# Norms without a shift folded into weights and outputs: x transposed instead of the normalised h

## The chip, the cores and the metric

The kernel runs on 1 core of one Trainium2 chip. The metric is the device time of one execution in microseconds; a comparison uses the median of several runs. The profile is one execution recorded by the hardware profiler.

## What is computed

256 rows of 1024 numbers, x, go through two blocks, each two layers deep. A layer of the first block is an FFN, a token mixer with three branches (retention, latent attention, differential attention), cross attention to a memory, and a second FFN. The second block has adaptive norms, a hybrid mixer and a mixture of experts; its parts stay as they are. What matters here is the norm ahead of each part of the first block:

```python
def rms_norm(x, gain=None):
    y = xf * lax.rsqrt(jnp.mean(xf * xf, axis=-1, keepdims=True) + EPS)
    if gain is not None:
        y = y * gain
...
for l in range(DEPTH):
    h = rms_norm(x, ffn1_norms[l, 0])
    x = x + 0.5 * rms_norm(swiglu(h, ffn1_w13[l], ffn1_w2[l]), ffn1_norms[l, 1])
    h = rms_norm(x, mix_norms[l, 0])
    y = token_mixing(h, w_in[l], ...)
    x = x + rms_norm(y, mix_norms[l, 1])
    h = rms_norm(x, cross_norms[l, 0])
    m = rms_norm(mem, cross_norms[l, 2])
    x = x + rms_norm(cross_attention(h, m, ...), cross_norms[l, 1])
    h = rms_norm(x, ffn2_norms[l, 0])
    x = x + 0.5 * rms_norm(swiglu(h, ffn2_w13[l], ffn2_w2[l]), ffn2_norms[l, 1])
```

In such a norm a row of x is multiplied by its own inverse root and then, column by column, by a gain. The result goes into a matrix product: h @ w.

## The kernel before

**Precision and weights.** Products are made in three passes of a 4-byte format: an operand is split into a high part and the low rest, and high x high, high x low and low x high are summed in PSUM (mm3, lines 288 to 290). Weights come from HBM in packages of 1 MB (mostly four k-slices of 128 rows and 512 columns) into one of four raw buffers. A class Stream holds the list of all packages in their order of use. Its pump splits them ahead of use into a ring of eight places (four tiles named hl, two tiles named pair that hold two splits each): ScalarE copies the slice into the high part (line 276), VectorE subtracts to get the low part (line 278). At a few packages, the first of a stage, every second low part is made by GpSimd instead. A place is free again when PE has done the matmuls of its split.

**Stages.** TensorE's order is written out by hand in the program's order; every engine takes its instructions in order. In a dense stage (dense) each k-slice gives six matmuls, three for each of the two tiles of 128 rows. After each stage's output product (dense_out) stands a boundary. At dense_out's end eight splits are kept: row tile 0 runs all of them first, and rest then gives out the eight parts of row tile 1 (three matmuls each) between the steps of the boundary.

**A boundary** (boundary, from line 516) does for each row tile: squares of the output y on ScalarE (line 444), y times its gain on VectorE (491, 493), the inverse root by a sum on VectorE (449) and a power on GpSimd (450), x plus the scaled y (496); this is add_post. Then pre_norm: squares of x (444), its root (449, 450), and h = x times root times gain (512). Then to_fm transposes h by eight matmuls against an identity (431) into two PSUM tiles, and hilo splits these: hh on ScalarE (282), hl on VectorE (283). Then the first projection of the next stage (staggered, 358 and 360) uses the eight splits of its first two packages: for each half of four k-slices, eight matmuls with hh and then four with hl. It runs wholly for row tile 0, and then for row tile 1, whose pre_norm and transposes stand in between. The order of calls for row tile 0: add_post, pre_norm, the last five parts of rest, transposes. The gain of each norm comes by a DMA that spreads one row over 128 partitions.

Between mix and cross attention, a boundary hands its steps to a filler: they are issued between the k-slices of the memory's projections. The boundaries into the second block have a shift in their norm.

**Stages ahead and behind.** An FFN has eleven blocks of its up projection (w13) with SiLU and a product (696, 697); in eight of them VectorE also accumulates the modulation vectors of the second block (1310, 1312). Mix copies projections from PSUM by evacuate (731), has sigmoids (1043, 1095), and normalises the latent vectors (qn, 875) before they are transposed (431).

## Time and profile before

| what | value |
|---|---|
| median of 3 runs | 2259.35 us (2256.45 to 2260.48) |
| profiled execution, its own time | 2260.74 us |
| its span, first to last instruction | 2258.9 us |
| mean granted TensorE clock | 0.976 |
| busy: PE, DVE, ACT, POOL | 94%, 60%, 49%, 5% |
| HBM read | 554.14 MB |

PE is TensorE with its matmuls, PEld its weight loads, DVE VectorE, ACT ScalarE, POOL GpSimd. A row of the timeline has its start, its length, the engine, the line, the operation, what is written and read, the number of instructions merged, and in brackets the idle time before it and what ended it. A row of groups has the count, the busy time and the mean of one in ns. The waits say which line waited for which. The stage table has one row for each stretch of time.

### The profile page before, as it was taken

The numbers are of one execution on the slowest core, as the hardware profiler recorded it, in microseconds if no ns is written. First come the engines' busy times: TensorE is split into PE (matmuls) and PEld (weight loads), VectorE is DVE, ScalarE is ACT, GpSimd is POOL, SyncE is SP. The second block draws the span as 40 slices with busy tenths as digits, with TensorE's granted clock in tenths as the row PEclk, the third lists the DMA queues.
The fourth block names the chain that finished last, engine by engine and source line by source line (L and its number), as shares of the span: only waits on it lengthen the run. The fifth ranks groups of instructions, "written<-read, shape, count | busy, mean of one in ns | idle before, by whom it ended". The sixth has DMA issues, their size and how long they took to land. (4 is left out here: it accounts for less than half of the span.)

```text
span 2258.9 us, 28926 instructions
## 1 busy us (share of the span) xinstructions
PE 2122.5 (94%) x10668; PEld 1565.5 (69%) x10668; DVE 1347.0 (60%) x2468; ACT 1097.0 (49%) x2194; POOL 103.1 (5%) x100
## 2 busy tenths in 40 slices
PE   7999999999999999999999999998989886999885
PEld 6887878888788788777788878876765333775341
DVE  5876667764776677676678568766562114563111
ACT  5544666565554455465756555545842112753110
POOL 1001000000100100010000010002000001000000
PEclk9999999999999999999999999999999798999998
DMA  8875534553576577744356437766479998568998
GB/s 287 310 246 188 210 117 167 202 196 128 207 282 241 197 273 259 255 175 150 132 196 212 166 118 273 259 239 239 165 285 377 419 420 314 217 228 340 419 418 344
DMA packets 95705, 557.26 MB, mean 247 GB/s; under 512 B 11096, under 2 KB 13083, under 8 KB 42551
## 3 DMA queue, kind: packets, MB, share of 16 engines
q1 hardware_dynamic: 95550, 555.28, 66.4%
q8 instruction: 88, 1.44, 0.3%
q14 instruction: 67, 0.54, 0.1%
HBM read 554.14 MB, written 1.10 MB: 246 GB/s over the span
## 5 line engine op out<-in xcount | busy, mean ns | idle before, releaser
L278 DVE TENSOR_TENSOR hl<-raw,hl 128x512 fp32r<-128x512 f32 (+2 forms) x586 | 392.5, 685 | 129.9 <-ACT hl L276 124.5
L276 ACT ACTIVATE hl<-raw 128x512 fp32r<-128x512 f32 (+1 forms) x602 | 366.2, 627 | 206.8 <-PE y L290 62.4
L278 DVE TENSOR_TENSOR pair<-raw,pair 128x512 fp32r<-128x512 f32 (+2 forms) x468 | 305.0, 692 | 125.6 <-ACT pair L276 121.1
L276 ACT ACTIVATE pair<-raw 128x512 fp32r<-128x512 f32 x484 | 276.8, 622 | 184.4 <-PE gu L290 69.3
L1921 PE MATMUL gu<-raw,xg 128*32 128x512 f32 x1024 | 144.3, 635 | 28.3 <-DMA raw<-w_gu 26.4
L288 PE MATMUL gu<-pair,hh 128*128 128x512 f32 x320 | 127.6, 399 | 0.0
L288 PE MATMUL gu<-hl,hh 128*128 128x512 f32 x320 | 127.5, 398 | 0.0
L290 PE MATMUL gu<-hl 128*128 128x512 f32 x320 | 125.7, 393 | 0.0
L290 PE MATMUL gu<-pair,hl 128*128 128x512 f32 x320 | 125.1, 391 | 0.0
L289 PE MATMUL gu<-pair,hh 128*128 128x512 f32 x320 | 124.8, 390 | 0.0
L289 PE MATMUL gu<-hl,hh 128*128 128x512 f32 x320 | 124.8, 390 | 0.0
L1312 DVE SCALAR_TENSOR_TENSOR ada<-raw,cact,ada 128x512 f32<-128x512 f32 x168 | 122.2, 746 | 0.0
L1921 PEld LDWEIGHTS gu<-raw,xg 128*32 128x32 f32 x1024 | 29.7, 111 | 109.3 <-DMA raw<-w_gu 55.9
L1908 PEld LDWEIGHTS gather<-P,u 128*128 128x128 f32 x512 | 70.7, 218 | 29.2 <-issue 20.0
L1978 PE MATMUL dn<-raw,aT 128*32 128x512 f32 x512 | 77.9, 622 | 9.9 <-ACT xg L1913 2.8
L1961 DVE SCALAR_TENSOR_TENSOR sil<-sil,cs,gu 128x256 f32<-128x256 f32 x16 | 7.7, 480 | 127.4 <-ACT sil L1960 127.2
L1908 PE MATMUL gather<-P,u 128*128 128x128 f32 x512 | 76.5, 308 | 3.3 <-DVE xg L1915 1.9
L283 DVE TENSOR_TENSOR y<-dn,y 128x512 fp32r<-128x512 f32 x32 | 22.1, 692 | 92.7 <-ACT y L282 92.6
L450 POOL TENSOR_TENSOR rs<-rs_tmp,mhalf 128x1 f32<-128x1 f32 x44 | 25.6, 581 | 1131.2 <-DVE rs_tmp L449 1122.7
L1913 ACT ACTIVATE xg<-gather,fm 128x128 f32<-128x128 f32 x64 | 29.3, 457 | 98.3 <-PE gather L1908 83.8
L288 PE MATMUL y<-hl,ah 128*128 128x512 f32 x184 | 73.4, 399 | 0.0
L1915 DVE TENSOR_SCALAR xg<-gather,fm 128x128 f32<-128x128 f32 x64 | 26.2, 410 | 78.1 <-ACT xg L1913 74.0
(663 smaller groups left out, 4730.5 us busy)
## 6 DMA issues: line engine op xcount, KB each, us to landing
raw<-w SPq DMA_DIRECT2D x131, 1024.0 KB
raw<-w_gu SPq DMA_DIRECT2D x98, 1024.0 KB
raw<-win SPq DMA_DIRECT2D x71, 1024.0 KB
raw<-w_dn SPq DMA_DIRECT2D x54, 1024.0 KB
raw<-w_ada SPq DMA_DIRECT2D x48, 1024.0 KB
raw<-w_gu SPq DMA_DIRECT2D x60, 512.0 KB
raw<-w_out SPq DMA_DIRECT2D x16, 1024.0 KB
raw<-cross_wkv SPq DMA_DIRECT2D x16, 1024.0 KB
```

Of the source, the lines that this page charges most:

```text
L276: nc.scalar.activation(hi, raw[:, c0:c0 + n], AF.Copy)
L278: eng.tensor_tensor(out=lo, in0=raw[:, c0:c0 + n], in1=hi.bitcast(F32), op=ALU.subtract)
L288: te.matmul(out, xh, wh, start=start, stop=False)
L289: te.matmul(out, xh, wl, start=False, stop=False)
L290: te.matmul(out, xl, wh, start=False, stop=stop)
L450: self.nc.gpsimd.tensor_tensor(out=out, in0=tmp, in1=self.mhalf[:, 0:1], op=ALU.pow)
L1312: nc.vector.scalar_tensor_tensor(self.ada[:, c], w, act, self.ada[:, c], op0=ALU.mult, op1=ALU.add)
L1908: te.matmul(ps[:, (k - k0) * 128:(k - k0 + 1) * 128], hm[t][:, k * 128:(k + 1) * 128], P[t][:, q * 128:(q + 1) * 128], start=(t == 0), sto ...
L1913: nc.scalar.activation(xg[:, k, :], v, AF.Identity, bias=sh, scale=g)
L1915: ve.tensor_scalar(xg[:, k, :], v, g, sh, op0=ALU.mult, op1=ALU.add)
L1921: te.matmul(gu[32 * e:32 * e + 32, :], xg[:, k, 32 * e:32 * e + 32], w(e), start=(k == 0), stop=(k == 7))
L1978: te.matmul(dn[half][32 * e:32 * e + 32, :], aT[:, f, 32 * e:32 * e + 32], w(e), start=(f == 0), stop=(f == 1))
```

## The change

For the norms without a shift whose output goes into a product (FFN1, FFN2, mix and cross of both layers), h is no longer made. The gain of a norm belongs to the k rows of the weight. A table of all these gains, g_pre (128 x 64), is loaded once, and a split of w13, win, win_mla or cross_wq multiplies with its column: ScalarE's copy gets it as a scale vector, and VectorE computes raw times gain minus high part in one instruction. GpSimd makes none of these splits. The root of a row tile belongs to the rows of the product; it is put into a small tile, pre (128 x 2), and multiplied in where the projections leave PSUM: as the scale vector of SiLU, sigmoid, copies and squares, and in the product behind SiLU. In mix the latent's root is multiplied with it once more. x itself is transposed and split. The norm of the memory and the norms of the second block stay.

The order in a boundary changes too: x of row tile 0 is transposed after seven of the eight parts of rest, and the squares and roots of both tiles stand behind the transposes of tile 1.

```diff
+NORMED = {"w13_1": 0, "w13_2": 1, "win": 2, "win_mla": 2, "cross_wq": 3}
...
+            name, index, pool = self.keys[i]
+            gain = None
+            if name in NORMED:
+                k = 16 * NORMED[name] + 8 * index[0] + 4 * (index[1] % 2) + s
+                gain = self.kern.g_pre[:, k:k + 1]
+            self.ready.append((i, self.kern.split(place, self.raws[i], c0, w, pool and self.emitted % 2, gain)))
...
+        if gain is not None:
+            nc.scalar.activation(hi, raw[:, c0:c0 + n], AF.Copy, scale=gain)
+            nc.vector.scalar_tensor_tensor(lo, raw[:, c0:c0 + n], gain, hi.bitcast(F32), op0=ALU.mult, op1=ALU.subtract)
+            return hi, lo
...
+        fold = gn == FOLDED
+        if fold:
+            self.pre = self.small.tile([128, 2], F32, tag="pre", name="pre", bufs=2)
         def pre_of(t):
-            if gn is not None:
+            if fold:
+                ms = self.small.tile([128, 2], F32, tag="ms", name="ms")
+                for i, c in enumerate(HALF):
+                    self.square_sum(ms[:, i:i + 1], self.x[t][:, c], D, tiles[t][0][:, c])
+                self.rstd2(self.pre[:, t:t + 1], ms)
+            elif gn is not None:
                 self.pre_norm(self.x[t], gn[0], gn[1], *tiles[t])
...
-            self.to_fm(tiles[t][1], hT[t], 8)
+            self.to_fm(self.x[t] if fold else tiles[t][1], hT[t], 8)
...
-        pre_of(0)
-        rest(2, 2)
-        rest(4)
-        post_of(1)
-        o0 = out_of(0)
+        if fold:
+            rest(2, 2)
+            rest(3)
+            out_of(0)
+            rest(1)
+            post_of(1)
+        else:
...
-        pre_of(1)
+        if not fold:
+            pre_of(1)
         out_of(1)
+        if fold:
+            pre_of(0)
+            pre_of(1)
         run(1)
...
+        self.g_pre = cp.tile([128, 64], F32, name="g_pre")
+        nc.sync.dma_start(self.g_pre, a["g_pre"])
...
-                    nc.scalar.activation(sil[:, t, :], ps[t][:, 0:256], AF.Silu)
-                    nc.vector.tensor_mul(act[:, t, :], ps[t][:, 256:512], sil[:, t, :])
+                    nc.scalar.activation(sil[:, t, :], ps[t][:, 0:256], AF.Silu, scale=rs[:, t:t + 1])
+                    nc.vector.scalar_tensor_tensor(act[:, t, :], ps[t][:, 256:512], rs[:, t:t + 1], sil[:, t, :],
+                                                   op0=ALU.mult, op1=ALU.mult)
...
+            nc.vector.tensor_mul(rs, rs, pr_rs.unsqueeze(2).to_broadcast([128, 2, 2]))
```

The order of PE at the boundary from FFN1 to mix in layer 0, before (y_1296 and y_1297 are the two halves of row tile 1's output, first_1802 is the first projection of row tile 0):

```order
L290 MATMUL y_1296<-hl,al_1289 128x512
L288 MATMUL y_1297<-hl,ah_1288 128x512
L289 MATMUL y_1297<-hl,ah_1288 128x512
L290 MATMUL y_1297<-hl,al_1289 128x512
L431 MATMUL tp<-ident,h 128x128 x8
L358 MATMUL first_1802<-pair,hh 128x512 x8
```

The same place after the change (y_1289 and y_1290 are the halves of tile 1's output, x_85 is row tile 0 of x, first_1787 its projection):

```order
L303 MATMUL y_1289<-hl,al_1284 128x512
L444 MATMUL tp<-ident,x_85 128x128 x8
L301 MATMUL y_1290<-hl,ah_1283 128x512
L302 MATMUL y_1290<-hl,ah_1283 128x512
L303 MATMUL y_1290<-hl,al_1284 128x512
L371 MATMUL first_1787<-pair,hh 128x512 x8
```

The transposes moved ahead of the last three matmuls of the old stage, and read x.

VectorE's order at this boundary before, from the sum that completes row tile 0 of x on (x_85 and x_86 are the row tiles of x, y_1296 and y_1297 the output of tile 1):

```order
L496 SCALAR_TENSOR_TENSOR x_85<-u,rs,x_85 128x512 x2
L278 TENSOR_TENSOR pair<-raw,pair 128x512
L449 TENSOR_SCALAR rs_tmp<-ms 128x1
L512 SCALAR_TENSOR_TENSOR h<-x_85,rs,gain 128x512 x2
L278 TENSOR_TENSOR pair<-raw,pair 128x512
L491 TENSOR_TENSOR u<-y_1296,gain 128x512
L449 TENSOR_SCALAR rs_tmp<-ms 128x1
L493 TENSOR_TENSOR u<-y_1297,gain 128x512
L283 TENSOR_TENSOR hl<-tp,hh 128x512 x2
L278 TENSOR_TENSOR hl<-raw,hl 128x512
L496 SCALAR_TENSOR_TENSOR x_86<-u,rs,x_86 128x512 x2
L278 TENSOR_TENSOR hl<-raw,hl 128x512
```

And after the change:

```order
L509 SCALAR_TENSOR_TENSOR x_85<-u,rs,x_85 128x512 x2
L287 SCALAR_TENSOR_TENSOR pair<-raw,g_pre,pair 128x512 x3
L296 TENSOR_TENSOR hl<-tp,hh 128x512 x2
L504 TENSOR_TENSOR u<-y_1289,gain 128x512
L462 TENSOR_SCALAR rs_tmp<-ms 128x1
L506 TENSOR_TENSOR u<-y_1290,gain 128x512
L287 SCALAR_TENSOR_TENSOR pair<-raw,g_pre,pair 128x512
L287 SCALAR_TENSOR_TENSOR hl<-raw,g_pre,hl 128x512
L509 SCALAR_TENSOR_TENSOR x_86<-u,rs,x_86 128x512 x2
L287 SCALAR_TENSOR_TENSOR hl<-raw,g_pre,hl 128x512 x3
L296 TENSOR_TENSOR hl<-tp,hh 128x512 x2
L462 TENSOR_SCALAR rs_tmp<-ms 128x1 x2
```

The two scalings of h are gone, all eight low parts of the weights are here (of the eight before, four stood on GpSimd), and three of them now come ahead of the low part of x. At the boundary from cross attention to FFN2, four come ahead; before the change it was two on VectorE there:

```order
L509 SCALAR_TENSOR_TENSOR x_85<-u,rs,x_85 128x512 x2
L287 SCALAR_TENSOR_TENSOR hl<-raw,g_pre,hl 128x512
L287 SCALAR_TENSOR_TENSOR pair<-raw,g_pre,pair 128x512 x2
L296 TENSOR_TENSOR hl<-tp,hh 128x512 x2
L504 TENSOR_TENSOR u<-y_4733,gain 128x512
L462 TENSOR_SCALAR rs_tmp<-ms 128x1
L506 TENSOR_TENSOR u<-y_4734,gain 128x512
L287 SCALAR_TENSOR_TENSOR pair<-raw,g_pre,pair 128x512 x2
L509 SCALAR_TENSOR_TENSOR x_86<-u,rs,x_86 128x512 x2
L287 SCALAR_TENSOR_TENSOR hl<-raw,g_pre,hl 128x512 x2
```

The first of the four stands one row ahead of this piece; the two last low parts come behind x of row tile 1, as at the other boundary.

More of the change, by code (lines that the diff above doesn't have):

```diff
@@ L36 @@
 SPLITS = 8
+FOLDED = "in the weights"
 RAWS = ["raw%d" % i for i in range(4)]
@@ L172, in __init__ @@
         self.slots, self.used, self.pair = deque(["hl"] * SPLITS2 + PAIRS), deque(), None
-        self.items = [(i, c0, n) for i, key in enumerate(self.keys)
-                      for c0, n in SEGMENTS.get(key[0], [(j * 512, 512) for j in range(4)])]
+        self.items = [(i, s, c0, n) for i, key in enumerate(self.keys)
+                      for s, (c0, n) in enumerate(SEGMENTS.get(key[0], [(j * 512, 512) for j in range(4)]))]
         self.emitted = 0
@@ L216, in pump @@
             last = self.emitted + 1 == len(self.items) or self.items[self.emitted + 1][0] != i
-            self.ready.append((i, self.kern.split(place, self.raws[i], c0, w, self.keys[i][2] and self.emitted % 2)))
+            name, index, pool = self.keys[i]
[4 more added lines that the diff above has]
+            self.ready.append((i, self.kern.split(place, self.raws[i], c0, w, pool and self.emitted % 2, gain)))
             self.emitted += 1
@@ L270, in load, with split @@
         return raw
-    def split(self, place, raw, c0, n, pool=False):
+    def split(self, place, raw, c0, n, pool=False, gain=None):
         nc = self.nc
         hi, lo = place[:, :n], place[:, 512:512 + n]
+        if gain is not None:
+            nc.scalar.activation(hi, raw[:, c0:c0 + n], AF.Copy, scale=gain)
+            nc.vector.scalar_tensor_tensor(lo, raw[:, c0:c0 + n], gain, hi.bitcast(F32), op0=ALU.mult, op1=ALU.subtract)
+            return hi, lo
         nc.scalar.activation(hi, raw[:, c0:c0 + n], AF.Copy)
@@ L469, in pre_load @@
         if pre[0] == "norm":
-            return self.gain(pre[1]), None
+            return FOLDED
         l, i = pre[1:]
@@ L546, in boundary @@
         rest(1, 1)
-        pre_of(0)
-        rest(2, 2)
-        rest(4)
-        post_of(1)
-        o0 = out_of(0)
+        if fold:
[6 more added lines that the diff above has]
+            pre_of(0)
+            rest(2, 2)
+            rest(4)
+            post_of(1)
+            out_of(0)
         self.st.pump(2)
@@ L867, in mix @@
             rs = sm.tile([128, 2, 2], F32, tag="mrs", name="mrs", bufs=1)
+            sc = sm.tile([128, 2, 2], F32, tag="msc", name="msc", bufs=1)
+            for j, n in enumerate((256, 128)):
+                nc.vector.tensor_scalar_mul(sc[:, :, j], pr_rs, n ** -0.5)
             for t in range(2):
-                self.square_sum(ms[:, t, 0:1], ps[t][:, 0:256], 256)
-                self.square_sum(ms[:, t, 1:2], ps[t][:, 256:384], 128)
-                nc.scalar.activation(kr[:, t, 0, :], ps[t][:, 384:416], AF.Copy)
+                for j, c in enumerate((slice(0, 256), slice(256, 384))):
+                    junk = self.junkp.tile([128, 256], F32, tag="junk", name="junk")[:, :c.stop - c.start]
+                    nc.scalar.activation(junk, ps[t][:, c], AF.Square, scale=sc[:, t, j:j + 1], accum_out=ms[:, t, j:j + 1])
+                nc.scalar.activation(kr[:, t, 0, :], ps[t][:, 384:416], AF.Copy, scale=pr_rs[:, t:t + 1])
             self.rstd(rs.rearrange("p a b -> p (a b)"), ms.rearrange("p a b -> p (a b)"))
+            nc.vector.tensor_mul(rs, rs, pr_rs.unsqueeze(2).to_broadcast([128, 2, 2]))
             for t in range(2):
@@ L1042, in mix @@
             for t in range(2):
-                nc.scalar.activation(rg[:, t, :], ps[t], AF.Sigmoid)
-                nc.vector.tensor_mul(rg[:, t, :], ps[t], rg[:, t, :])
+                nc.scalar.activation(rg[:, t, :], ps[t], AF.Sigmoid, scale=pr_rs[:, t:t + 1])
+                nc.vector.scalar_tensor_tensor(rg[:, t, :], ps[t], pr_rs[:, t:t + 1], rg[:, t, :],
+                                               op0=ALU.mult, op1=ALU.mult)
             def ret_pairs():
@@ L1189, in cross @@
             values(0)
-            to_T(qT, "cross_wq", 0, lhs, "q0")
+            to_T(qT, "cross_wq", 0, lhs, "q0", rs=self.pre)
             ot = []
@@ L1249, in cross @@
                    for t in range(2)]
[L1250 removed]
+            to_T(qT, "cross_wq", 1, lhs, "q1", rs=self.pre)
             self.spawn(when("q1", heads((2, 3))))
@@ L2031, in body @@
                 self.cb = self.pool("const1")
-                h, ps = self.boundary(None, lambda n, pump=0: self.st.pump({1: 0, 2: 0, 4: 2}[n]), None, None, gain,
-                                      first=pair("w13_1", 0))
+                h, ps = self.boundary(None, None, None, None, FOLDED, first=pair("w13_1", 0))
                 self.nc.scalar.activation(self.cact, self.cact, AF.Silu)
```

34 lines of the change are left out of this document (19 added, 15 removed).

## The prediction

> **What bounds the kernel now.** I read the engines' shares first, then PE's waits, then the stages, then single boundaries in the timeline. The page's first part gives the bound:
>
> ```profile
> PE 2122.5 (94%) x10668; PEld 1565.5 (69%) x10668; DVE 1347.0 (60%) x2468; ACT 1097.0 (49%) x2194; POOL 103.1 (5%) x100
> ```
>
> TensorE is the bound, so time can only come from its idle time. Its list of waits names the lines that the change touches (us in total, times, longest):
>
> ```profile
> PE tp L431 <- DVE h L512: 20.8, 9, 10.7
> PE first L358 <- DVE hl L278: 7.4, 4, 2.0
> PE first L358 <- DVE pair L278: 4.6, 4, 2.0
> ```
>
> L431 transposes the normalised h, L512 writes it, L358 is the first projection of a stage and L278 the low half of a weight split. 10.7 of the 20.8 us is one wait, at the program's start. The stage table (length, then busy time of PE, PEld, DVE, ACT, POOL, granted clock, DMA share, GB/s) says where PE does not wait: the first mix, and the up projections of the first FFN that also feed the modulation vectors. The last two rows are slices of the two boundaries behind cross attention:
>
> ```profile
> 226.00:435.00 209.00, 208.36 (x1055) 170.47 (x1054) 147.27 (x319) 132.03 (x309) 4.29 (x3) 1.00 0.48 170
> 33.00:118.00 85.00, 85.00 (x388) 69.01 (x387) 68.22 (x123) 40.86 (x78) 0.00 (x0) 1.00 0.85 305
> 582.00:586.00 4.00, 4.00 (x17) 3.40 (x17) 1.87 (x3) 1.19 (x2) 0.00 (x0) 0.66 0.84 340
> 1334.00:1338.00 4.00, 2.47 (x11) 2.10 (x12) 4.00 (x7) 2.11 (x7) 2.01 (x2) 0.70 0.12 14
> ```
>
> So inside a stage PE never waits; what can be won lies at the start and at five boundaries (FFN1 to mix and cross to FFN2 in both layers, FFN2 to FFN1 between them). The two mix-to-cross boundaries are covered by the memory projections, and the boundaries into the second block are not folded. For the five, here are the last matmul of the old stage and the first dense one of the new:
>
> ```profile
> 207.22 0.39 PE L290 MATMUL y<-hl,al 128*128 128x512 f32 x1
> 208.67 1.29 PE L431 MATMUL tp<-ident,h 128*128 128x128 f32 x8 [1.06 <-DVE h L512]
> 212.58 0.50 PE L358 MATMUL first<-pair,hh 128*128 128x512 f32 x1 [0.71 <-POOL pair L278]
> 217.12 0.97 PE L358 MATMUL first<-hl,hh 128*128 128x512 f32 x3 [1.95 <-DVE hl L278]
> 226.02 0.35 PE L288 MATMUL mla<-pair,hh 128*128 128x416 f32 x1
> 569.11 0.39 PE L290 MATMUL y<-hl,ol 128*128 128x512 f32 x1
> 580.00 0.96 PE L358 MATMUL first<-hl,hh 128*128 128x512 f32 x3 [1.76 <-DVE hl L278]
> 589.89 0.40 PE L288 MATMUL gu<-hl,hh 128*128 128x512 f32 x1
> 769.62 0.39 PE L290 MATMUL y<-pair,al 128*128 128x512 f32 x1
> 788.59 0.39 PE L288 MATMUL gu<-pair,hh 128*128 128x512 f32 x1
> 968.18 0.39 PE L290 MATMUL y<-hl,al 128*128 128x512 f32 x1
> 987.93 0.35 PE L288 MATMUL mla<-hl,hh 128*128 128x416 f32 x1
> 1332.51 0.40 PE L290 MATMUL y<-pair,ol 128*128 128x512 f32 x1
> 1352.81 0.40 PE L288 MATMUL gu<-hl,hh 128*128 128x512 f32 x1
> ```
>
> Start to start they take 18.80, 20.78, 18.97, 19.75 and 20.30 us. The work in between is 16 transposes and 48 matmuls (0.23 us apart, as 217.12 shows), some 13.5 us.
>
> **Prices of the new instructions.** Rows for the shapes used:
>
> ```profile
> L276 ACT ACTIVATE hl<-raw 128x512 fp32r<-128x512 f32 x590 | 360.9, 630 | 198.1 <-PE y L290 62.4 <-PE gu L290 31.0 <-DVE hl L278 26.6
> L444 ACT ACTIVATE u<-x 128x512 f32<-128x512 f32 x48 | 30.1, 628 | 35.0 <-DVE x L496 23.6 <-DVE x L1738 5.6 <-DVEq L2001 4.1
> L1787 ACT ACTIVATE u<-x,rs x8: 705/710/721, 1676.2 to 2040.4; 128x512 f32<-128x512 f32 x8
> L278 DVE TENSOR_TENSOR hl<-raw,hl 128x512 fp32r<-128x512 f32 x574 | 386.6, 688 | 122.3 <-ACT hl L276 116.9
> L1312 DVE SCALAR_TENSOR_TENSOR ada<-raw,cact,ada 128x512 f32<-128x512 f32 x168 | 122.2, 746 | 0.0
> L496 DVE SCALAR_TENSOR_TENSOR x<-u,rs,x 128x512 f32<-128x512 f32 x32 | 34.9, 1132 | 0.3
> ```
>
> 592 splits (88 w13 packages, 48 win, 4 win_mla, 8 cross_wq, four each) become longer: ACT with a scale vector as L1787, 710 against 630 ns, +47 us in all; DVE as L1312, 746 against 688 ns, +34 us. Both lie beside PE: in the up projections DVE goes from 68.22 of 85 us to about 72 (60 splits, +0.06 each), so the cover stays. Were it gone, PE would pay; that is the third rival. The scaled evacuations (SiLU, sigmoid, copies) add some 0.08 us each to work that is consumed steps later: nothing. The gain loads that go, 7 of 0.5 MB, leave a queue with DMA to spare at these places; only the first is on the path.
>
> **A boundary, step by step** (FFN1 to mix, layer 0). Rows of ACT and DVE:
>
> ```profile
> 203.68 1.42 DVE L496 SCALAR_TENSOR_TENSOR x<-u,rs,x 128x512 f32<-128x512 f32 x2
> 206.77 2.42 DVE L512 SCALAR_TENSOR_TENSOR h<-x,rs,gain 128x512 f32<-128x512 f32 x2 [0.66 <-POOL rs L450]
> 209.33 1.26 ACT L282 ACTIVATE hh<-tp 128x512 fp32r<-128x512 f32 x2 [1.00 <-PE tp L431]
> 213.00 3.46 DVE L496 SCALAR_TENSOR_TENSOR x<-u,rs,x 128x512 f32<-128x512 f32 x2
> ```
>
> x of row tile 0 is done at 205.10, h only at 209.19. In the new order PE transposes x before the last three of the y matmuls, at 206.75, where x has been there for 1.6 us: the first wait goes. The last y matmuls hide ACT's hh (209.33 is 0.66 us after the transposes' start, so 207.4 now), and the projection starts at 208.6. What is late next is the lower half of the splits. Three are made before the transposes; the fourth stands on ACT behind hh and the two squares of y (0.7 us each with their accumulator's read, L444 being 628 ns), so its high half ends near 210.8. On DVE follow, at 0.6 to 0.7 us each: hl of x twice to 209.3, u, the root's input, u to 210.95, the fourth low half to 211.65, the fifth to 212.35, x of tile 1 twice to 213.75, the sixth to eighth to 215.8. PE, 0.23 us a matmul: six matmuls to 210.0, wait for the fourth split, to 211.95; low pass to 212.85; waits for the sixth to eighth split, to 216.1; low pass to 217.0; transposes and hh 1.3 us as 208.67 to the next matmul; tile 1's 24 matmuls 5.6 us: 223.9. From 207.2 that is 16.7 us, 2.1 less than now. Contention is in favour: L496 takes 3.46 for two while POOL splits, 1.42 alone, and POOL has no split left here.
>
> FFN2 to FFN1 has the same three early splits: 18.97 - 16.7 = 2.3. In the other three boundaries four splits come early, so the first half (12 matmuls) runs without a wait, and only the seventh and eighth low half are late, by 1.7 and 0.4 us: by the same count from the last y matmul +1.4 for its end, +2.8, +5.0, +1.3, +5.6 = 16.0 us. Gains: 20.78 - 16.0 = 4.8; 19.75 - 16.0 = 3.8; 20.30 - 16.0 = 4.3. Together with the two above 17.3 us.
>
> In those gains sits a loss of clock: PE's clock fell to 0.66 and 0.70 in a 4 us slice of the two cross boundaries, 1.4 and 1.2 us of PE; in the first of them no single wait is longer than the 1.76 at 580.00. Since a wait of 1.7 us remains, I count one of the two dips as staying: 17.3 - 1.3 = 16.0. [...]
>
> **The start.**
>
> ```profile
> GB/s 0 0 49 262 383 169 153 180 153 240 240 333 410 410 448 421 394 467 388 432 428 393 475 371 350 388 355 415 311 371 459 393 240 98 0 0 0 0 175 273
> 9.94 1.41 DVE L512 SCALAR_TENSOR_TENSOR h<-x,rs,gain 128x512 f32<-128x512 f32 x2 [4.58 <-DMA gain<-g_ffn]
> 14.87 2.19 ACT L276 ACTIVATE pair<-raw 128x512 fp32r<-128x512 f32 x4 [0.49 <-DMA raw<-w]
> 16.10 3.12 POOL L278 TENSOR_TENSOR pair<-raw,pair 128x512 fp32r<-128x512 f32 x2 [0.28 <-ACT pair L276]
> 20.67 1.29 PE L431 MATMUL tp<-ident,h 128*128 128x128 f32 x8
> 27.64 0.40 PE L288 MATMUL gu<-hl,hh 128*128 128x512 f32 x1
> ```
>
> (The first row cuts 0 to 30 us in 40.) The 10.7 us wait for h goes, but PE then waits for weights: the second package lands at 14.87. Without the gain's 0.5 MB it lands earlier by 1.3 us at 410 GB/s, by 3.7 if the slow 4.5 us from 3.75 on are all its doing; I take 2.0, nearer to the lower, since g_pre's short rows take its place. The last low half came from POOL at 19.22, 4.35 us after landing; DVE alone needs 0.7 and four times 0.7, 3.6. The start gains 2.0 + 0.75 = 2.7 us, between 2.0 and 4.5.
>
> **Added on the path.** In mix the latent's roots get one DVE product more, and its squares and copies a scale vector:
>
> ```profile
> 237.81 1.39 DVE L875 SCALAR_TENSOR_TENSOR qn<-mla,mrs,gm 128x256 f32<-128x256 f32 x4 [1.13 <-POOL mrs L413]
> 239.16 0.49 PE L431 MATMUL tp<-ident,qn 128*128 128x128 f32 x3
> ```
>
> The first half of qn is there at 238.5, 0.7 before PE reads it; the chain grows by 0.2 (the product), 0.2 and up to 0.4 (scales): 0 to 0.4 us a layer, I take 0.4, so 0.8. New waits: SiLU and the copies wait on ACT for the root from POOL, with the next high halves queued behind. Four squares (0.63 each) now follow tile 1's hh, so the root comes some 3.4 us after it, and its first use after tile 1's 5.6 us of matmuls. Nothing.
>
> **Sum.** 16.0 + 2.7 - 0.8 = 17.9 us off the profiled execution's 2260.74 (span 2258.9 and 1.84 around it): 2242.8. The median of the runs is 1.4 lower, 2259.35, so 2241.5.
>
> **The rivals.**
> - *Given back inside the stages.* Every split is longer, and in mix a dozen reads by PE have under 0.7 us to spare, like qn. At 0.3 us for a dozen in each of two layers 7 us are lost, and 2248.5 is left. For it: ACT and DVE are in-order queues. Against it: PE's busy 208.36 of 209 shows slack nearly everywhere.
> - *The wait only moves.* The longest wait at the boundary, 1.95 us, is for a low half on DVE, and DVE now makes the four that POOL made, 2.8 us. If that chain sets the end, boundaries stay as long as they are, and only the start's 2.7 - 0.8 remains: 2257, no change. Against it: DVE loses four scalings of h (2.42 for two above) and the contention.
> - *Slower: DVE becomes the bound of the up projections.* With 60 splits in 85 us it decides from (85 - 68.22) / 60 = 0.28 us more a split, 0.97 us. At L496's mean of 1.132 the stage takes 68.22 + 60 x 0.44 = 95, 10 us more, four times 40, so 2282. For it: no row has this form with an fp32r output. Against it: L1312 reads raw in the same stage at 746 ns, and L496 is slow only beside POOL.
>
> **How the numbers follow.** Forecast 0.60; given back 0.17; the wait moves 0.14; slower 0.06; 0.03 for more than all bounds at their best, 17.3 + 4.5 = 21.8 us. The low end is those 21.8 with 1.5 for rounding, 2236. The high end, 2255, takes in the first rival and lies 2 short of the second; the second and third are the 2 in 10 left out. About 0.2% (4.5 us) is what a measurement of this kernel tells from no change. Faster: forecast, first rival and the rest, 0.80; same 0.14; slower 0.06.
>
> **What would show it.** Right: no wait of tp for h; waits of the first projection for DVE low halves only, of 1 to 2 us; last y to first dense near 16 to 17 us at five places; the first dense matmul at 25 instead of 27.6; PE without waits in 33 to 118; ACT splits near 710, DVE splits near 750 ns. Wrong: DVE splits above 950 ns or waits for them inside the up projections (third rival), boundaries still at 19 us (second), scattered PE waits in mix (first).

## The result, and the profile after

The changed kernel takes 2234.75 us (median of 4 runs, 2232.35 to 2237.57) against 2259.91 for the kernel before (4 runs, 2256.45 to 2262.33): ratio 0.9885, 95% interval 0.9873 to 0.9897. That is 25.2 us less; the forecast was 17.9 us less, 2241.5, and its range began at 2236. The profiled execution took 2237.57 (span 2235.6), 23.2 less than that of before.

Waits of TensorE after the change, from the view that groups them (engine, line waited for: us in total, times, longest):

```profile
PE tp L444 <- DVE h L527: 9.2, 4, 6.1
...
PE first L371 <- DVE hl L287: 4.2, 5, 1.3
...
PE tp L444 <- DVE qn L919: 1.9, 2, 1.1
...
PE first L371 <- DVE pair L287: 1.8, 2, 1.3
...
PE first L371 <- ACT hh L295: 1.5, 6, 0.3
```

The first row is the two boundaries into the second block's layers, which the change leaves alone. At the five folded ones no transpose waits for h. In its place stand waits of the first projection: for low halves on DVE, 1.3 us at the longest, and short ones, 0.3 us at most, for ACT's hh. The prediction expected 1 to 2 us, and low halves only. The row of qn is new and lies inside mix.

The groups of the scaled splits, from the page (busy us, mean ns of one):

```profile
L287 DVE SCALAR_TENSOR_TENSOR hl<-raw,g_pre,hl 128x512 fp32r<-128x512 f32 (+1 forms) x296 | 214.1, 744 | 46.4 <-ACT hl L286 45.9
L286 ACT ACTIVATE hl<-raw,g_pre 128x512 fp32r<-128x512 f32 (+1 forms) x296 | 204.3, 719 | 62.3 <-PE gu L303 23.6
```

744 and 719 ns against 746 and 710 in the forecast. Now the boundary from FFN1 to mix in layer 0, TensorE first, then VectorE (start, us, engine, line):

```profile
25.22 0.39 PE L301 MATMUL gu<-hl,hh 128*128 128x512 f32 x1
...
140.83 0.40 PE L301 MATMUL y<-hl,ah 128*128 128x512 f32 x1
...
203.59 1.04 PE L444 MATMUL tp<-ident,x 128*128 128x128 f32 x8
205.15 1.54 PE L371 MATMUL first<-pair,hh 128*128 128x512 f32 x6
...
210.83 1.82 PE L371 MATMUL first<-hl,hh 128*128 128x512 f32 x5 [0.54 <-DVE hl L287]
...
220.28 0.35 PE L301 MATMUL mla<-pair,hh 128*128 128x416 f32 x1
...
1508.59 0.40 PE L303 MATMUL y<-hl,al 128*128 128x512 f32 x1
```

```profile
204.86 1.29 DVE L296 TENSOR_TENSOR hl<-tp,hh 128x512 fp32r<-128x512 f32 x2 [0.97 <-ACT hh L295]
206.06 0.68 DVE L504 TENSOR_TENSOR u<-y,gain 128x512 f32<-128x512 f32 x1
206.66 0.20 DVE L462 TENSOR_SCALAR rs_tmp<-ms 128x1 f32<-128x1 f32 x1
206.78 0.68 DVE L506 TENSOR_TENSOR u<-y,gain 128x512 f32<-128x512 f32 x1
207.38 0.74 DVE L287 SCALAR_TENSOR_TENSOR pair<-raw,g_pre,pair 128x512 fp32r<-128x512 f32 x1
208.04 0.75 DVE L287 SCALAR_TENSOR_TENSOR hl<-raw,g_pre,hl 128x512 fp32r<-128x512 f32 x1
208.70 1.41 DVE L509 SCALAR_TENSOR_TENSOR x<-u,rs,x 128x512 f32<-128x512 f32 x2
210.03 2.07 DVE L287 SCALAR_TENSOR_TENSOR hl<-raw,g_pre,hl 128x512 fp32r<-128x512 f32 x3
```

The prediction counted a boundary from the last y matmul of the old order, 0.46 us behind the new start of the transposes: 204.05 to 220.28, 16.23 us, where 16.7 was forecast and 18.80 stood before. The five in order: 16.23, 15.57, 16.23, 15.61, 15.56, together 79.2 against 98.6. The page's L509 is L496 of before; beside no work of POOL its two take 1.41 us, where two took 3.46. The first and last TensorE rows serve below: projections of FFN1 begin at 25.22 (27.64 before), and the last y matmul of layer 1 starts at 1508.59 (1532.28 before). The latter is called **the end of the block** below; 23.7 us of the difference lie ahead of it.

The clock, from windows over two boundaries (us, PE busy and instructions, granted clock, DMA share, GB/s), of before:

```profile
577.00:581.00 4.00, 2.20 (x8) 1.00 0.53 204
581.00:585.00 4.00, 4.00 (x15) 0.57 0.99 350
...
1336.00:1340.00 4.00, 3.84 (x13) 0.62 0.53 145
```

and of the changed kernel at the first of these places:

```profile
567.00:571.00 4.00, 2.75 (x11) 1.00 0.76 289
```

The clock stays at 1.00 there and in every other window over the five boundaries.

| | forecast | measured |
|---|---|---|
| wait of tp for h at the five boundaries | none | none |
| boundaries, us | 16.7 (two), 16.0 (three) | 16.23 (two), 15.56 to 15.61 (three) |
| clock dips that stay | 1 | 0 |
| first dense matmul | 25 | 25.22 |
| qn waits, two layers together | 0.8 | 1.95 |
| FFN stages, each | no change | 0.6 to 0.9 us shorter |

The last line was in no term. First dense matmul to last y of the old order was 179.47 to 179.73 before and is 178.83 to 178.84 now, with no wait in either.

### The profile page after: what moved, and what is told of

The parts are those of the page before. It is cut to its first block, busy times and chain, and to the rows that moved or that the text cites. A ratio compares the mean times of both kernels' runs of the same rounds, so it can differ in the third digit from the quotient of the medians.

```text
span 2235.6 us, 28877 instructions
## 1 busy us (share of the span) xinstructions
PE 2117.0 (95%) x10668; PEld 1566.0 (70%) x10668; DVE 1355.1 (61%) x2466; ACT 1156.2 (52%) x2194; POOL 67.7 (3%) x76
## 3 DMA queue, kind: packets, MB, share of 16 engines
HBM read 549.98 MB, written 1.10 MB: 247 GB/s over the span
## 5 line engine op out<-in xcount | busy, mean ns | idle before, releaser
L291 DVE TENSOR_TENSOR hl<-raw,hl 128x512 fp32r<-128x512 f32 (+2 forms) x302 | 203.3, 688 | 74.0 <-ACT hl L289 70.6
L289 ACT ACTIVATE hl<-raw 128x512 fp32r<-128x512 f32 (+1 forms) x306 | 186.9, 626 | 111.2 <-PE y L303 53.7
L287 DVE SCALAR_TENSOR_TENSOR hl<-raw,g_pre,hl 128x512 fp32r<-128x512 f32 (+1 forms) x296 | 214.1, 744 | 46.4 <-ACT hl L286 45.9
L286 ACT ACTIVATE hl<-raw,g_pre 128x512 fp32r<-128x512 f32 (+1 forms) x296 | 204.3, 719 | 62.3 <-PE gu L303 23.6
L287 DVE SCALAR_TENSOR_TENSOR pair<-raw,g_pre,pair 128x512 fp32r<-128x512 f32 (+1 forms) x296 | 207.6, 744 | 45.7 <-ACT pair L286 43.3
L286 ACT ACTIVATE pair<-raw,g_pre 128x512 fp32r<-128x512 f32 (+1 forms) x296 | 196.6, 716 | 71.6 <-PE gu L303 50.9
L1966 PE MATMUL gu<-raw,xg 128*32 128x512 f32 x1024 | 144.9, 638 | 26.8 <-DMA raw<-w_gu 25.2
L291 DVE TENSOR_TENSOR pair<-raw,pair 128x512 fp32r<-128x512 f32 (+1 forms) x184 | 119.8, 692 | 69.7 <-ACT pair L289 69.3
L289 ACT ACTIVATE pair<-raw 128x512 fp32r<-128x512 f32 (+1 forms) x188 | 107.4, 621 | 91.5 <-PE y L303 64.3
```

What stands on the lines that cost most here:

```text
L286: nc.scalar.activation(hi, raw[:, c0:c0 + n], AF.Copy, scale=gain)
L287: nc.vector.scalar_tensor_tensor(lo, raw[:, c0:c0 + n], gain, hi.bitcast(F32), op0=ALU.mult, op1=ALU.subtract)
L289: nc.scalar.activation(hi, raw[:, c0:c0 + n], AF.Copy)
L291: eng.tensor_tensor(out=lo, in0=raw[:, c0:c0 + n], in1=hi.bitcast(F32), op=ALU.subtract)
L1966: te.matmul(gu[32 * e:32 * e + 32, :], xg[:, k, 32 * e:32 * e + 32], w(e), start=(k == 0), stop=(k == 7))
```

## The experiments

The theory when they began: the five boundaries were sized about right and for the right reason, h no longer stands ahead of the transposes; some 3 us come from the FFN stages, for an unknown reason. The rivals: the gain lies in something that went along with h (POOL's halves, the gain load, the order), or the pace of the stages has nothing to do with the arithmetic.

**What the scaled splits cost.** e1_unscaled; the output lacks the four pre-norm gains:

```
-            if name in NORMED:
+            if name in ():
```

> The changed kernel with plain weight splits (ACT copies, DVE subtracts; the four pre-norm gains are left out of the computation), all else as changed. Theory A (the scaled forms cost nothing where they stand, and the 0.7 us that each feed-forward stage has become shorter comes from elsewhere): time within 2 us of the changed kernel's 2234.8, boundaries 15.6 to 16.2 us, up-projection blocks stay at 11.37 us. Theory B (the DVE chain of low halves sets the boundary's end): 0.06 us less a low half, 4 to 5 of them late, so 0.3 us less at each of five boundaries, 1.5 us less in all. Theory C (the pace of the up projections comes from the form of the DVE split): blocks go back to 11.42 to 11.48, each feed-forward stage to 179.6, about 3 us more, 2238.

Measured: 2237.69 us, ratio 0.9895 (0.9878 to 0.9911). The FFN stages kept their short length (first dense to first y matmul 115.61 us as in the changed kernel), so theory C falls: the form of the split isn't the pace. Three boundaries became 0.24 to 0.3 us shorter, as theory B says. But the two into mix became 3.2 and 2.4 us longer, which no theory said. The plain form has a branch to POOL that the scaled one lacks, and the keys of win still ask for it. Rows of VectorE there:

```profile
205.81 1.73 DVE L291 TENSOR_TENSOR hl<-raw,hl 128x512 fp32r<-128x512 f32 x1
207.47 3.45 DVE L509 SCALAR_TENSOR_TENSOR x<-u,rs,x 128x512 f32<-128x512 f32 x2
```

and of POOL:

```profile
206.96 3.42 POOL L291 TENSOR_TENSOR hl<-raw,hl 128x512 fp32r<-128x512 f32 x2
```

Each DVE instruction beside POOL's takes 1.73 us, the time of one of POOL's (1.71), instead of 0.7. TensorE's clock fell to 0.50 at both places too (208.21 to 215.04 and 962.56 to 965.97), so a part of the 3.2 and 2.4 us is clock. The run was thus an unplanned trial of POOL's halves, repeated without them as e9_unscaled_no_pool (gains left out as in the first):

```
-        keys = [("win", (l, i), i < 2) for i in range(2)]
+        keys = [("win", (l, i), False) for i in range(2)]
```

> The first experiment again (plain splits, the four pre-norm gains left out of the computation), but with no low half on POOL at the mix boundaries either, where the plain form had fallen back to POOL for four of them. Theory A (the scaled forms are hidden everywhere but in the chain of low halves at the boundaries): all five boundaries 0.25 to 0.3 us shorter than the changed kernel's, stages unchanged, time 1.3 us under 2234.8, 2233.5. Rival (what was longer in the first experiment at the mix boundaries, 18.6 and 17.1 us from the last y matmul instead of 15.4 and 14.7, was not POOL): they stay long.

Measured: 2231.65 us, ratio 0.9882 (0.9866 to 0.9899). The boundaries are 15.92 and 15.32 us, 1.4 us less in all than the changed kernel's, and those into mix are short again. Theory A for the boundaries, and POOL it was. The scaled form costs about 0.3 us a boundary in the chain of low halves. Against theory A it isn't hidden everywhere else: the two stages of mix and cross are 0.46 and 0.41 us shorter than the changed kernel's.

**POOL's halves alone.** The kernel before, moved like e6 below, with one part of the change: e10_before_no_pool takes POOL's halves from win and w13:

```
-            keys += [("w13_" + which, (l, 2 * j + i), j == 0) for i in range(2)]
+            keys += [("w13_" + which, (l, 2 * j + i), False) for i in range(2)]
-        keys = [("win", (l, i), i < 2) for i in range(2)]
+        keys = [("win", (l, i), False) for i in range(2)]
```

> The kernel before, tiles moved by 64 B as in the run that gave 2256.4, with one part of the change alone: no low halves of splits on POOL ahead of the two projections of FFN and mix (DVE makes all). Theory A (POOL's halves slow DVE beside them, 3.46 us against 1.42 for two of L496, and that is a part of the boundary's gain): waits of 1.95 for DVE halves shrink, the clock dips at mix and FFN2 to FFN1 boundaries become fewer, 1 us a boundary there and 0.75 at the start, 2253. Rival (POOL relieved DVE): DVE's chain is 2.8 us longer, the boundaries grow by 0.7 each, 2259.

Measured: 2241.95 us, ratio 0.9926 (0.9909 to 0.9942); that is 14.5 us under its sister with POOL (e6, 2256.43; the kernel before differed by 1.2 us between the two series), where 3 were expected. TensorE at the boundary into mix:

```profile
205.82 1.29 PE L431 MATMUL tp<-ident,h 128*128 128x128 f32 x8
...
210.72 0.50 PE L358 MATMUL first<-pair,hh 128*128 128x512 f32 x1 [1.68 <-DVE pair L278]
...
1515.87 0.40 PE L290 MATMUL y<-hl,al 128*128 128x512 f32 x1
```

and VectorE, the pair that took 3.46:

```profile
211.18 1.41 DVE L496 SCALAR_TENSOR_TENSOR x<-u,rs,x 128x512 f32<-128x512 f32 x2
```

The transposes still read h, and the norm stands in the chain as ever, yet here they don't wait for it: h of tile 0 takes 1.41 instead of 2.42 us. All five boundaries are 17.54 to 17.73 us, 11.4 less together than in the sister, with no clock dip. Ahead of the end of the block (1527.81 in the sister) lie 11.9 us of the 14.5. The rest lies in the stages behind, which this edit does not touch: they take 723.7 us here and 726.3 in the sister, and anything from 720.8 to 729.7 in the profiles of all kernels but e12.

**The order of the transposes.** e2_late_transposes:

```
-            rest(3)
-            out_of(0)
-            rest(1)
+            rest(4)
+            out_of(0)
```

> The changed kernel, but PE transposes x of row tile 0 after the last y matmuls instead of three matmuls ahead of them. Theory A (that order hides ACT's high halves of x under the last y matmuls): the first projection waits 1.0 to 1.3 us more for hh, boundaries at 16.6 to 17.3 us, five times 1.0: about 2240. Rival (the first projection waits for DVE's low halves of the weights anyway, so an earlier start buys nothing): boundaries and time as changed, 2234.8 within 1.5.

Measured: 2237.96 us, ratio 0.9901 (0.9884 to 0.9917). Rows of TensorE into mix, layer 0:

```profile
202.46 1.04 PE L444 MATMUL tp<-ident,x 128*128 128x128 f32 x8
203.75 1.65 PE L371 MATMUL first<-pair,hh 128*128 128x512 f32 x6 [0.25 <-ACT hh L295]
```

The cover lost is small: from one first dense matmul to the next, FFN1 and its boundary take 195.81 us against 195.06. Four boundaries lost 0.57 to 0.75; at the fifth, into mix of layer 1, the clock fell and 2.1 us went:

```profile
958.22:961.63 3.41, 2.09 (x7) 1.00 0.53 211
961.63:965.04 3.41, 3.41 (x12) 0.50 0.68 231
```

Theory A in kind, smaller in size.

**The start.** e3_gain_load_back:

```
+                self.gain(gn("g_ffn1", 0, 0)[1])
                 self.open_splits(keys + self.mix2_keys(0), 2)
```

> The changed kernel with the 0.5 MB gain load put back at the start, its result used by nothing. Theory A (of the start's gain 2.0 us come from that load): second weight package lands 2 us later, first dense matmul at 27.2 instead of 25.22, time 2236.8. Rival (the start's gain comes from h not being waited for, or from POOL's low halves going): first dense matmul within 0.5 us of 25.2, time unchanged.

Measured: 2238.03 us, ratio 0.9895 (0.9878 to 0.9911). TensorE waits 3.42 us instead of 1.29 for the first high half, which itself waits for its weights:

```profile
12.19 4.14 PE L371 MATMUL first<-hl,hh 128*128 128x512 f32 x8 [3.42 <-ACT hl L286]
```

First dense matmul at 27.09, 1.9 later: theory A. Without the load it lies between 23.38 and 25.40 in eleven kernels, so the term is 1.7 to 3.7 us, and the changed kernel's own 25.22 is among the later ones.

**The latent's root.** e4_latent_root:

```
                 self.rstd2(self.pre[:, t:t + 1], ms)
+                ev = self.pre_ev[:, t:t + 1]
+                self.nc.vector.tensor_scalar(ev, ms[:, 0:1], ms[:, 1:2], EPS, op0=ALU.add, op1=ALU.add)
+                self.nc.vector.tensor_scalar_mul(ev, ev, EPS)
...
-                    nc.scalar.activation(junk, ps[t][:, c], AF.Square, scale=sc[:, t, j:j + 1], accum_out=ms[:, t, j:j + 1])
+                    nc.scalar.activation(junk, ps[t][:, c], AF.Square, scale=(256, 128)[j] ** -0.5, accum_out=ms[:, t, j:j + 1])
...
-            self.rstd(rs.rearrange("p a b -> p (a b)"), ms.rearrange("p a b -> p (a b)"))
-            nc.vector.tensor_mul(rs, rs, pr_rs.unsqueeze(2).to_broadcast([128, 2, 2]))
+            nc.vector.tensor_add(ms, ms, pr_ev.unsqueeze(2).to_broadcast([128, 2, 2]))
+            nc.gpsimd.tensor_tensor(out=rs.rearrange("p a b -> p (a b)"), in0=ms.rearrange("p a b -> p (a b)"),
+                                    in1=self.mhalf[:, :4], op=ALU.pow)
```

> The changed kernel with another form of the latent's root: plain squares of the projection, and (ms + eps * (mean x^2 + eps))^-1/2 as the whole scale, so that neither a scaled square nor a product with the row's root stands in the chain (the same result in exact arithmetic). Theory A (the 0.87 and 1.08 us that PE waits for qn in the two mix stages are that chain): the waits fall to 0.2 or less, time 1.5 us less, 2233.2. Rival (something behind it is as late): the wait turns up at a later instruction of mix, the stage stays at 343.5 and 345.4 us, time unchanged.

Measured: 2235.63 us, ratio 0.9889 (0.9872 to 0.9905): no gain to be seen. The waits for qn are gone, but all FFN stages had grown by 0.6 to 0.9 us, with their code untouched: first dense to first y matmul 116.35 us instead of 115.61, and 116.36 in before. What this kernel shares with before is a place: its small tiles differ, so its first working buffer starts 160 bytes above a multiple of 256 within each partition, as in before; in the changed kernel and the first three experiments it starts 224 above one.

**The place of the tiles.** Four kernels with an unused tile of n bytes a partition ahead of x (64, 64, 64 and 96):

```
+        pad = cp.tile([128, n // 4], F32, name="pad")
+        nc.gpsimd.memset(pad, 0.0)
         self.mhalf = cp.tile(
```

> The changed kernel with an unused 64 B (per partition) tile ahead of x, so that every later tile lies 64 B higher. Before and the run with the other latent root start their first buffer at 32 mod 128 and ran PE slowly (stages FFN1 of 179.1 to 179.6 us, 0.2292 us a matmul in 40 to 140 us); the changed kernel and three runs with 96 mod 128 ran it fast (178.37 us, 0.2278). Theory P (the place of the tiles sets PE's pace): this kernel, at 32 mod 128, gets the slow pace in all its stages, FFN1 and FFN2 at 179.1 to 179.3 us, 3 to 5 us more in all, 2238 to 2240. Rival (the pace differs from execution to execution): it is not tied to the place; FFN stages at 178.4, time 2235.

> The kernel before with the same unused 64 B tile, nothing else. Theory P: its first buffer is now at 96 mod 128, so it gets the fast pace: FFN stages about 0.7 us shorter each (178.8 instead of 179.6 from the first dense matmul to the last of the old order), 3 to 5 us less, 2255 to 2257, ratio 0.998. Rival (execution to execution): as before, 2260, ratio 1.000.

> The other form of the latent's root, with the unused 64 B tile, so that its tiles lie where those of the changed kernel lie. Theory P with the waits for qn gone: stages of mix and cross 0.9 to 1.1 us shorter than the changed kernel's 343.0 and 344.9, FFN stages at 178.37, so 2 us less than the changed kernel: 2232.5. Rival (execution to execution): the pace may be either; time as its sister without the tile, 2235.6.

> The same with a 96 B tile: the first buffer at a multiple of 128 (and of 512). Theory P says only that the pace follows the place, so FFN stages either at 178.4 or at 179.1, the same for all four of them; a third value would show more than two paces. Rival: as in the other three, no tie.

Measured: e5 2240.34 us, ratio 0.9911 (0.9893 to 0.9928), 5.6 more than the changed kernel; e6 2256.43, ratio 0.9981 (0.9971 to 0.9991), 2.0 to 6.6 less than before by the interval, 4.3 by the medians; e7 2230.59, ratio 0.9866 (0.9845 to 0.9886); e8 2241.86, ratio 0.9916 (0.9895 to 0.9938), the same code as e7 32 bytes further on. Theory P four times, though with more than two paces: the FFN stages of e5 and e8 take 179.9 to 180.5 us, longer than any before. First dense and first y matmul of e5:

```profile
24.11 0.39 PE L301 MATMUL gu<-hl,hh 128*128 128x512 f32 x1
...
141.37 0.40 PE L301 MATMUL y<-hl,ah 128*128 128x512 f32 x1
```

of e6, and its end of the block:

```profile
27.24 0.39 PE L288 MATMUL gu<-hl,hh 128*128 128x512 f32 x1
...
142.85 0.40 PE L288 MATMUL y<-hl,ah 128*128 128x512 f32 x1
...
1527.81 0.40 PE L290 MATMUL y<-hl,al 128*128 128x512 f32 x1
```

117.26 us for e5; 115.61 for e6, as the changed kernel's 140.83 - 25.22. All four FFN stages of e6 are 178.84 us long: what the changed kernel's stages gained is the place, to 0.01 us. e6 also shows where dips begin. It had four, before had two. Here the windows are cut where the granted clock changes: the four dips, two of them with the window ahead, and the window from 975.25, which no dip followed:

```profile
214.08:217.49 3.41, 1.54 (x7) 1.00 0.69 207
217.49:220.90 3.41, 3.41 (x13) 0.50 0.65 271
569.06:572.48 3.42, 1.44 (x10) 1.00 0.00 0
572.48:575.89 3.41, 3.41 (x10) 0.50 0.72 226
777.28:780.69 3.41, 3.41 (x12) 0.50 0.87 279
975.25:978.66 3.41, 1.88 (x7) 1.00 0.23 36
1333.65:1337.06 3.41, 3.41 (x10) 0.50 0.73 226
```

Each dip is 3.41 us at half the clock, 1.71 us of TensorE's time; the 0.57 and 0.62 above are windows cut otherwise, with some full clock in them. The starts of the four lie 354.99, 204.80 and 556.37 us apart, which is 104, 60 and 163 times 3.413; the two of before (581.29 and 1335.64) lie 221 times that apart. So within an execution the clock changes on one grid of 3.413 us, and the grid lies elsewhere in each (2.45 us behind a multiple of 3.413 in e6, 1.02 in before).

In e7 the waits for qn are gone and the place is the changed kernel's: mix and cross are 1.1 and 1.4 us shorter (341.89 and 343.55 from the first dense matmul to the transposes; 343.01 and 344.91). Its TensorE reads qn without a wait:

```profile
232.69 0.49 PE L444 MATMUL tp<-ident,qn 128*128 128x128 f32 x3
```

It is the fastest complete kernel here, 4.2 us under the changed one by the medians; the two intervals overlap. Then three more places (128 bytes on before; 32 and 224 on the latent form):

> The kernel before with an unused 128 B tile: its first buffer lies at 32 mod 256, where the changed kernel moved by 64 B ran at 0.2311 us a matmul (40 to 140 us). Theory P (the pace is a function of the place, the same for both kernels): 0.231 here too, FFN stages 0.4 to 0.6 us longer than in the unmoved one, 2262 to 2264. Rival (each kernel has its own accidents): anything from 0.2277 to 0.2295, 2256 to 2260.

> The other form of the latent's root, first buffer at 192 mod 256, a residue not seen yet (224 gave 0.2278 us a matmul and 2230.6, 160 gave 0.2292 and 2235.6, 0 gave 0.2304 and 2241.9). Theory P says that the time follows the pace at all of them, about 4 us for 0.001 us: at 0.2278 2231, at 0.2304 2241. By neighbours (160 and 224) 0.228 to 0.229, 2231 to 2235. Rival: the time does not follow the pace.

> The same at 128 mod 256. If the pace is a function of the place mod 256 that changes smoothly, 0.229 to 0.230 and 2235 to 2240; if it depends on the place mod 128 alone, as at 0: 0.2304 and 2241. Rival: the time does not follow the pace.

Measured: e14 2262.09 us, ratio 1.0017 (1.0008 to 1.0027); e15 2241.25, ratio 0.9929 (0.9913 to 0.9946); e16 2246.26, ratio 0.9947 (0.9928 to 0.9966). The tie of pace and place holds: e14 has e5's pace to 0.01 us though the kernels differ. The time follows the pace less closely: e16 is 4.4 us above e8 by the medians, but its block ends only 2.1 us later, and its five runs range from 2239.53 to 2250.19.

```profile
27.53 0.39 PE L288 MATMUL gu<-hl,hh 128*128 128x512 f32 x1
...
144.79 0.40 PE L288 MATMUL y<-hl,ah 128*128 128x512 f32 x1
```

The guesses by neighbours were wrong: it isn't smooth, and 192 is slow.

| start of the first working buffer, mod 256 | first dense to first y matmul of FFN1, us | kernels |
|---|---|---|
| 224 | 115.61 to 115.67, once 116.04 | changed, e1, e2, e3 (116.04), e6, e7, e9 to e13 |
| 160 | 116.35, 116.36 | e4, before |
| 0 | 117.00 | e8 |
| 192 | 117.09 | e15 |
| 128 | 117.17 | e16 |
| 32 | 117.26, 117.26 | e5, e14 |

In the 116.04 of e3 no wait shows either, and the clock is 1.00; why it is longer stays open.

**Either half of the fold.** e11_gain_folded_only:

```
+            self.pre = self.ones2
...
+                self.rstd2(rs, ms)
+                for c in HALF:
+                    self.nc.vector.tensor_scalar_mul(tiles[t][1][:, c], self.x[t][:, c], rs)
...
-            self.to_fm(self.x[t] if fold else tiles[t][1], hT[t], 8)
+            self.to_fm(tiles[t][1], hT[t], 8)
...
+        pre_of(0)
         rest(2, 2)
-            rest(3)
-            out_of(0)
-            rest(1)
+        rest(4)
         post_of(1)
+        out_of(0)
```

> Half of the change: the gains in the weights as changed, but the inverse root still multiplied into x ahead of the transposes (one product by a column instead of the product by root and gain), in the old order; the outputs are scaled by ones. Tiles lie as in the changed kernel. Theory A (what the boundary waits for is the root's chain and the late transposes): the wait of tp for h stays at 0.9 to 1.5 us, the transposes' cover is lost (0.65), some clock dips come back: boundaries 2 us longer than the changed kernel's, about 2245. Rival (it was the gain product and POOL that cost): 2237 or less.

Measured: 2241.84 us, ratio 0.9923 (0.9906 to 0.9939); e10, without any folding, took 2241.95, and the block ends at 1515.87 in both. Boundaries 17.18 to 17.36 us, 1.0 to 1.7 longer than the changed kernel's; tp waits for h only 0.34 to 0.41 us at three of them, and the clock does not fall. Theory A had the sign, and 7 of its 10 us, but not the parts: no dip came back, and the wait for h is a small one. At the boundary into mix the price is a later chain of low halves, whose eighth ends 8.87 us behind the start of the last y matmul (213.11 - 204.24) instead of 8.05 (212.10 - 204.05).

```profile
205.91 1.88 PE L371 MATMUL first<-pair,hh 128*128 128x512 f32 x7 [0.39 <-ACT hh L295]
209.19 0.50 PE L371 MATMUL first<-pair,hh 128*128 128x512 f32 x1 [1.40 <-DVE pair L287]
```

e12_root_folded_only, the other half:

```
+        def scale(t):
+            for c in HALF:
+                self.nc.vector.tensor_mul(tiles[t][1][:, c], self.x[t][:, c], gn[1][:, c])
...
         rest(1, 1)
         if fold:
+            scale(0)
             rest(2, 2)
```

> The other half: the root at the outputs and the new order as changed, but the gains multiplied into x ahead of the transposes (two DVE products of 0.69 us a row tile, and the gain loads), plain splits, none on POOL. Tiles lie as in the changed kernel. Theory A (the DVE chain of low halves sets the boundary's end): h is in time for the transposes, but each low half behind is 1.4 us later, less 0.06 a plain split: boundaries 1.1 to 1.4 us longer, clock dips possible, and the start 2 us later for the gain load: 2242. Rival (the products are covered): boundaries as changed, only the start's 2 us: 2237.

Measured: 5752.85 us, ratio 2.55 (2.5424 to 2.5509). This kernel leaves out the product in the cross stage, whose boundary goes another way, and transposes a tile there that holds other data. The experts then get other loads (4096 matmuls of gather instead of 512), and the whole time tells nothing. Up to the end of the block, at 1509.59, the rows can be read: boundaries of 14.6 to 15.1 us from the last y matmul, as short as the changed kernel's. With the product there too, e13_root_folded_only_mended:

```
-            filler([lambda: post_of(0), lambda: pre_of(0), lambda: post_of(1), lambda: pre_of(1),
+            filler([lambda: post_of(0), lambda: (scale(0), pre_of(0)), lambda: post_of(1), lambda: (scale(1), pre_of(1)),
```

> Root at the outputs and the new order as changed, gains multiplied into x ahead of the transposes (DVE, two products of 0.69 us a row tile, and the gain loads), plain splits, none on POOL; now with the product in the cross stage too, which the run before lacked. Tiles lie as in the changed kernel. Theory A (root and order hold the 7 us beyond POOL's halves, and the products are hidden, as the boundaries of the run before showed): boundaries 15.0 and 14.6 us, only the start 2 us later: 2235 to 2237. Rival (the gains' half counts): 2240 to 2242, like the run with the gains alone.

Measured: 2233.80 us, ratio 0.9896 (0.9880 to 0.9913). TensorE:

```profile
27.40 0.39 PE L301 MATMUL gu<-hl,hh 128*128 128x512 f32 x1
...
205.78 1.03 PE L444 MATMUL tp<-ident,h 128*128 128x128 f32 x8
...
222.16 0.35 PE L301 MATMUL mla<-pair,hh 128*128 128x416 f32 x1
...
1509.60 0.40 PE L303 MATMUL y<-hl,al 128*128 128x512 f32 x1
```

Theory A: 2.2 us later at the start for its gain load, 1.2 less in the rest of the block, and the changed kernel's time. The two products a tile are hidden. What the gains in the weights bring is the start; about half of it goes back in the boundaries (0.3 us) and the two mix stages (1.0), where e9 showed the price of the longer splits.

## Why the prediction was wrong in size and right in kind

Three terms of the sum were too small: nothing stood for the place of the tiles (4.3 us), the boundaries' gain was 2.1 short, and a clock dip of 1.3 was kept that did not stay. In mix it went the other way: 1.15 more for qn than forecast, and 1.1 of further waits.

*Where the 23.7 us to the end of the block come from*, at the kernels that part them: 4.5 from the place (before to e6, though e6 has two clock dips more), 11.9 from POOL's halves (e6 to e10, the four dips included), 7.3 from the rest of the change (e10 to the changed kernel: 1.4 at the start and 8.8 at the boundaries, less 2.9 in mix and cross).

*The place: the term that was missing.* The sum had nothing for tiles that move, and g_pre and the two root tiles move all behind them by 320 bytes. Worth 4.3 us by the medians, 2.0 to 6.6 by the interval. At equal place the change is worth 21.7 us (2256.43 to 2234.75); had the tiles stayed in place, the changed kernel would by this have taken 2239.0, 2.5 under the forecast and inside its range. The forecast put this term at nothing without a reason.

*The boundaries, 17.3 us: right in mechanism, 2.1 too small.* 19.4 profile to profile. The step that failed is the count on DVE "at 0.6 to 0.7 us each": from the transposes' start the eighth low half was put at 9.05 us (215.8 - 206.75) and came at 8.51 (212.10 - 203.59). Up to the low halves of x the count fits (2.55 us, and 206.15 - 203.59 = 2.56). Then u, the root's input and u took 1.31 us (206.15 to 207.46) where 1.65 stood, since the root's input is an instruction of 0.20 us. The rest took 4.64 (to 212.10) where 4.85 stood, since DVE starts a split 0.66 us after the one ahead of it, though each lasts 0.74 (208.04 - 207.38). Some 0.45 us at each of five.

*The kept dip, 1.3 us: wrong.* None stayed. The reason given, that a wait of 1.7 us remains, failed: the longest in the folded boundaries is 1.26. The size was off too: a dip is 1.71 us of TensorE's time, not 1.2 to 1.4. When one comes is settled in part. In e6 TensorE was busy 1.40 to 1.54 us in the windows of the grid ahead of the four dips, and 1.88 in the one from 975.25. In all profiles, from 100 us to 1540, a dip followed every window at full clock with under 1.59 us busy, and none with over 2.09. In between busy time alone does not decide: before has a dip behind 1.65 and none behind 1.66 (windows from 577.88 and 977.24). TensorE was busy for 38 to 61% of the windows that dips followed (1.31 us of 3.41 in before, from 1332.22; 2.09 in e2, from 958.22). That the grid of 3.413 us lies elsewhere in each execution would explain why a boundary dips in one and not in another, but no run tests that alone.

*What the boundaries' gain hung on: half right.* The text had POOL's contention as a remark "in favour", with no price. It was the largest single part, 11.9 us with the dips that came with it, and it also made h late. Where no dip stands, the boundaries with POOL's halves take 18.80 to 19.89 us (in before, e6 and e14) and those of e10 17.54 to 17.73: 1.2 to 2.3 us each. The rows of e1 show what POOL's halves do: a low half on DVE takes 1.73 us beside POOL's 1.71, and 0.69 in the mean of the changed kernel's page (L291, 688 ns). Why the one holds up the other, no run shows. The wait for h, on which the text built, goes to zero to 0.55 us by POOL's going alone (e10).

*The start, 2.7 us: about right.* 2.4 measured. The gain load is 1.7 to 3.7 (e3), and DVE in place of POOL 0.66 (first dense 27.24 in e6, 26.58 in e10), where 2.0 and 0.75 stood. Three slips in the text change little: 0.7 and four times 0.7 is 3.5 and not 3.6, the terms of the 16.0 add up to 16.1 as printed, and eight gain loads went, not 7 (HBM read 554.14 MB before, 549.98 after).

*The qn chain, -0.8 us: right in kind, -1.95 measured.* The upper end of 0.4 us a layer held the terms, but waits of 0.87 and 1.08 us came. The term that was missing is the scale vector of the squares, msc: it is made on DVE behind a low half of the splits, and ACT stands idle for it:

```profile
229.99 0.48 ACT L913 ACTIVATE junk<-mla,msc 128x256 f32<-128x256 f32 x1 [0.95 <-DVE msc L909]
```

In the second mix stage this is 1.05 us. e4 and e7, which need neither msc nor the product, have no wait for qn.

*Cover of the scaled splits: right.* No wait in the up projections; the third rival had DVE splits at 0.97 us, they take 0.744. The first rival shows in mix alone: its two stages with cross are 1.3 and 1.8 us longer than in e6 (343.47 and 345.37, against 342.21 and 343.58, from the first dense matmul to the old order's last y), of which qn is 1.95 in all.

Against 17.9 from the profiled executions: + 2.1 boundaries + 1.3 dip - 0.3 start - 1.15 qn + 3.0 FFN stages makes 22.9 of 23.2. Left out are, in mix and cross, 1.9 gained by the place and 1.1 lost in further waits, and 0.4 lost behind the block. The medians differ by 2 more because the changed kernel's profiled execution was the longest of its four.

## What to carry to other kernels

Ask of an engine that is taken off a stage what it did to its neighbour there: four halves on POOL looked like help and cost 2.3 us a boundary on the mean of five, clock dips included. The changed kernel still has them at the boundary into the second block: L509 takes 3.46 us there for two, and TensorE waits 1.97 us for a low half. Taking them off there was not tried. Ahead of a comparison that turns on a few tenths of a per cent, look whether tiles have moved, and run both kernels at the same place. Where a product is split off from a chain, test each factor alone: here the root with the new order, without POOL's halves, gave the whole time (e13), and the gains could have stayed in h.

## What the runs showed of the hardware

- TensorE's pace depends on where the tiles start: the same matmuls take 115.61 to 117.26 us by the start mod 256, with the clock granted at 1.00 and no wait, the same to 0.01 us for two different kernels at one place. That is 1.4%; over the kernel 2230.6 us (224) against 2235.6 (160), 2241.9 (0), 2241.3 (192) and 2246.3 (128) for one code. Which tile it hangs on, and why, was not tried.
- A two-input instruction on DVE (128x512, 4-byte) beside one on POOL took as long as POOL's: 1.73 us beside 1.71 (e1), instead of 0.7.
- TensorE's granted clock falls to 0.50 for 3.41 us or twice that (e1: 6.83), on a grid of 3.413 us within an execution, behind windows of that grid in which TensorE was busy for 1.30 to 2.09 us (up to 1540 us, all profiles).
